# A hybrid decoder step's projections as Strassen products of seven for eight, over pairs of column tiles

## The chip, the cores and the metric

The kernel runs on one core of one Trainium2 chip. The metric is the device time of one execution in microseconds (us). Before the change it is 1708.05 us, the median of three runs (1707.87 to 1709.57). All data are fp32 in DRAM. A core has a matrix engine (TensorE, PE in the profile; PEld is its weight load), three engines for elementwise work (VectorE or DVE, ScalarE or ACT, GpSimd or POOL) and SyncE (SP), whose queue issues the DMAs here. Each engine runs its own list of instructions strictly in order; semaphores hold it where it needs another's result.

## The reference, cut to what matters

One inference step of a decoder layer, for 1024 prompt tokens and 8 x 4 sample tokens together (1056 columns):

```
h = rmsnorm(x, g_norm)                    # x: 1056 tokens x 2048
P = h @ w_in                              # 2048 x 5904: columns of groups A, B, C, D
y_a = b * conv3(c * h_a) * silu(z_a)      # A: gated short convolution
y_b = rmsnorm(gla(q, k, v, decay)) * silu(z_b)          # B: gated linear attention, 4 heads
y_c = window_attention(q, k, v, sinks) * silu(z_c)      # C: window 128, 8 heads on 2 key heads
y_d = softmax(q mem_k) mem_v * silu(z_d)  # D: 256 memory tokens, 4 heads
y = x + concat(y_a, y_b, y_c, y_d) @ w_out              # 2048 x 2048
```

For the prompt the memory's keys and values are `rmsnorm(mem) @ w_mem_kv`; for the samples they come from caches, as do the earlier keys and states. New states and caches are outputs too.

## The kernel before

**Tiles.** Features lie on the 128 partitions, tokens along the free axis. The two projections have 46 column tiles of P (four of each part of A and so on) and 16 of the output. A column tile is 128 rows of P transposed, [128, 1056], in three chunks of 352 columns (`CW`), one PSUM bank each. k has 16 tiles of 128.

**Precision.** An fp32 operand is split in a high and a low part, in a format (fp32r) that TensorE takes in one pass: x into `xh` and `xl` (`load_x`, `split`), weights into `wh` (ACT, L344) and `wl` (POOL, mostly, L348). Three matmuls, wh xh + wl xh + wh xl, stand for one exact one (`products`, L369). So a column tile is 16 x 3 x 3 matmuls of 352 columns. A plain fp32 matmul appears in the trace as two records.

**Normalisation.** x is multiplied by `g_norm` when it is split. Its row norm R is known only once all of x is there; it is multiplied in where a chunk leaves PSUM (`to`, L414; `silu2`, L425).

**Stages.** `first_two` does D's first two query tiles while x arrives. `memory` does the memory's keys and values (L491). Then `tile_of` and `proj` do tile after tile: D's queries, a quarter of A, D's gates, C's keys, values and queries, a quarter of A, C's gates, and B in two halves, each with a quarter of A. Each finished feature of the mixer goes to `mix` in DRAM; in the last gate tile (`last_gate`) it is loaded and split again (L281, L282), taking x's place, and `output` does 16 tiles with the residual (L1314).

**What sets the order.** Attention runs in generators that stand in a queue (`_Pipe`). One step of each active one is issued before every twelve matmuls of a projection (`pipe.step()` in `proj`), so twelve steps go with a column tile. `pipe.drain()` issues all steps that are left, with no products between. The compiler's scheduler then orders each engine's instructions anew. Weights come as pieces [128, 512], loaded and split two pieces ahead (`take`).

**Names that the steps below use.** D: scores L599, low parts L636, output L627; its decode takes the cached keys `kc` (L673, loads L668) and values `vc` (L704, loads L698). C: `c_duo` does two blocks of two heads, scores L863, mask and maximum L871, exponent L883, division L891, transposes L900, output L911; then `c_decode`. B: `b_duo`, `b_blocks`, and `b_decode`, in which each sample's keys are picked (L1289), multiplied (L1293) and added to the state (L1295). L257 sums squares of x, L285 makes the low part of x, L434 applies a gate on POOL.

Of the kernel before, what the change touches and what calls it, by code (L numbers as in the profile page):

```python
# [22 lines left out]
CW = TOK // NCH  # L23
CG = TOK // 4
# [5 lines left out]
# Column tiles of the combined projection, and where their 128 columns lie in w_in.  # L30
# [13 lines left out]
def _columns():  # L44
# [7 lines left out]
    for j in range(2):  # L52
# [7 lines left out]
# Mixer features in the order in which their tiles are done.  # L60
MIX = ["A0", "D0", "D1", "D2", "D3", "A1", "C0", "C1", "C2", "C3",
       "A2", "B0", "B1", "A3", "B2", "B3"]
# [12 lines left out]
class _Pipe:  # L75
    """Work that fills in between the projections' products, in stages: each of its generators
    yields where the tensor engine would wait for the other engines."""
# [4 lines left out]
    def add(self, gen, alone=False, after=None, every=0, kind=None):  # L82
        """after: what must hold something before the generator starts; every: steps between the
        starts of those of a kind."""
        self.queue.append((gen, alone, after, every, kind))

    def step(self):
        self.t += 1
        left = []
        for gen, phase, alone in self.active:  # L90
# [4 lines left out]
        self.active = left  # L95
# [14 lines left out]
class _Step:  # L110
    def __init__(self, nc, tc, ctx, I, O):
# [4 lines left out]
        self.xp = e(tc.tile_pool(name="xp", bufs=KT))  # L116
        self.wp = e(tc.tile_pool(name="wp", bufs=3))
        self.rt = e(tc.tile_pool(name="rt", bufs=7))
        self.ct = e(tc.tile_pool(name="ct", bufs=4))
        self.sm = e(tc.tile_pool(name="sm", bufs=3))  # L120
        self.pj = e(tc.tile_pool(name="pj", bufs=4, space=PS))
        self.ms = e(tc.tile_pool(name="ms", bufs=4, space=PS))
        self.mix = tc.dram_tile([KT, P, TOK], F32, name="mix")
# [3 lines left out]
        self.xh, self.xl = [None] * KT, [None] * KT  # L127

# [7 lines left out]
    def ctile(self):  # L136
        return self.ct.tile([P, CW], F32, name=self.name("ct"), tag="ct")

    def ps(self, pool=None):
        if pool is self.pj:  # L140
            return self.pj.tile([P, 512], F32, name=self.name("pj"), tag="pj")
        return self.ms.tile([P, 512], F32, name=self.name("ms"), tag="ms")
# [5 lines left out]
    def take_constants(self):  # L148
# [30 lines left out]
        self.R = c.tile([P, TOK], F32, name="R")  # L179
# [10 lines left out]
    def masks(self):  # L190
        nc, c = self.nc, self.const
        # decode: [cached key, t]
# [4 lines left out]
        # gated linear attention: all ones where s <= t  # L197
# [6 lines left out]
        # the same for the sample group's chunks of 4, and which chunk a token is of  # L204
# [16 lines left out]
    def rsqrt(self, out, x, mult, eps, n):  # L221
        """out = 1 / sqrt(x * mult + eps) for a few columns."""
# [21 lines left out]
    def load_x(self):  # L244
        """Splits x * g_norm into two parts that one pass each carries; sums the squares."""
        nc = self.nc
        self.acc = [None] * 2
        last = None

        def square(k, xr):  # L250
            i = int(k % 4 == 3)
            nc.scalar.activation(xr, xr, AF.Square)  # L252
            if self.acc[i] is None:
                self.acc[i] = xr
            else:
                eng = nc.vector if i else nc.gpsimd
                eng.tensor_tensor(self.acc[i], self.acc[i], xr, op=ALU.add)  # L257
        for k in range(KT):
            xr = self.rtile("xr")
            parts = 1 if k else NCH  # L260
            w = TOK // parts
            for c in range(parts):
                s = slice(c * w, c * w + w)
                nc.sync.dma_start(out=xr[:, s], in_=self.I["xT"][k, :, s])
            self.split(k, xr, self.gn[:, k : k + 1], parts)
            if last:
                square(*last)
            last = k, xr
# [4 lines left out]
    def split(self, k, src, scale=None, parts=1):  # L273
        nc = self.nc
        h = self.xp.tile([P, TOK], F32R, name=self.name("xh"), tag="xh")
        l = self.xp.tile([P, TOK], F32R, name=self.name("xl"), tag="xl")
        w = TOK // parts
        for c in range(parts):
            a, b, d = (t[:, c * w : c * w + w] for t in (src, h, l))
            if scale is None:  # L280
                nc.scalar.copy(b, a)  # L281
                nc.vector.tensor_tensor(d, a, b.bitcast(F32), op=ALU.subtract)  # L282
            else:
                nc.scalar.activation(b, a, AF.Copy, scale=scale)  # L284
                nc.vector.scalar_tensor_tensor(d, a, scale, b.bitcast(F32), op0=ALU.mult,  # L285
                                               op1=ALU.subtract)
        self.xh[k], self.xl[k] = h, l

    def row_norms(self):
        """R[:, t] = 1 / rms(x_t), on every partition."""  # L290
# [5 lines left out]
        ps = self.ps(self.pj)  # L296
        nc.tensor.matmul(ps[:, 0:2], acc[:, TOK - P : TOK], self.ones[:, 0:2], start=True, stop=True)
        r = self.small(NB + 1, tag="rx")
        self.rsqrt(r[:, 0:NB], sums, 1.0 / D_MODEL, EPS, NB)
        self.rsqrt(r[:, NB : NB + 1], ps[:, 0:1], 1.0 / D_MODEL, EPS, 1)  # L300
        for g in range(3):
            ps = self.ps(self.ms if g == 1 else self.pj)
# [9 lines left out]
    # Weights pass through in pieces of 512 columns, in the order of self.pieces, loaded and split  # L312
    # ahead of the products that take them.
    def load_piece(self):
        nc = self.nc
        kind, src = self.pieces[len(self.raw)]
        n = len(self.raw)
        if kind == "m":
            # two pieces in one go
            wr = self.rtile("wm")  # L320
            nc.sync.dma_start(out=wr[:, 0:1024], in_=src)
            self.raw += [wr[:, 0:512], wr[:, 512:1024]]
            return
        if n < 8 and n % 2:
            wr = self.t5()
        else:
            wr = self.wp.tile([P, 512], F32, name=self.name("wr"), tag="wr", bufs=2)
        nc.sync.dma_start(out=wr, in_=src)
        self.raw.append(wr)

    def split_piece(self):
        nc = self.nc
        n = len(self.ready)
        kind, wr = self.pieces[n][0], self.raw[n]
        # while x arrives, and for the memory, every other piece lies where attention will
        if n < 8 and n % 2:
            wh, wl = self.r5(), self.r5()
        elif kind == "m" and n % 2:
            wh, wl = self.t5().bitcast(F32R), self.t5().bitcast(F32R)
        else:  # L340
            wh = self.wp.tile([P, 512], F32R, name=self.name("wh"), tag="wh")
            wl = self.wp.tile([P, 512], F32R, name=self.name("wl"), tag="wl")
# [4 lines left out]
        eng = nc.vector if n < 8 or (kind == "m" and n % 2) else nc.gpsimd  # L347
        eng.tensor_tensor(wl, wr, wh.bitcast(F32), op=ALU.subtract)  # L348
        self.ready.append((wh, wl))

# [12 lines left out]
    def products(self, ps, wh, wl, kq, c, kk):  # L363
# [8 lines left out]
    def proj(self, evac, after=None):  # L372
        """One column tile; work of the pipe comes in between."""
        ps = []
        for kq in range(4):
# [9 lines left out]
            if after:  # L385
                after(kq)
# [1143 lines left out]
```

## Time and profile before

| | |
|---|---|
| runs of the kernel | 1707.87, 1708.05, 1709.57 us |
| the profiled execution | span 1708.3 us |
| mean granted TensorE clock | 0.993 |
| L369, high by high, 2928 records | 329 ns each (they overlap) |
| HBM read and written | 111.18 MB and 19.66 MB |
| largest wait of PE | 7.9 us, for kc |

The durations of matmuls are modelled and overlap, so the distance between two starts says what one costs. A line `L369 PE MATMUL out<-in shapes xcount | busy, mean ns | idle before, releaser` is a group of instructions of one source line.

### The profile page before, as it was taken

The page shows a single profiled execution, that of the slowest core. Times are in us where ns is not written, and L with a number is a line of the kernel's source. Part 1 is how long each engine was busy: PE and PEld are TensorE (multiplying, and loading weights), DVE is VectorE, ACT ScalarE, POOL GpSimd, SP SyncE. Part 2 cuts the span into 40 slices and gives each one's busy share as a digit, 9 for nine tenths or more (in the row PEclk, how much of TensorE's full clock was granted, in tenths as well). Part 3 has the DMA queues.
Part 4 walks back from the last instruction along what each step waited for, and adds up shares of the span by engine and source line. Part 5 has one row for each costly group of instructions (what it writes and reads, how often), then busy time and mean ns, then how long its engine had stood idle before and what let it go on. Part 6 is the DMA issues. An engine that isn't in the chain of part 4 may idle for free.

```text
span 1708.3 us, 26563 instructions
## 1 busy us (share of the span) xinstructions
PE 1666.3 (98%) x10850; PEld 1593.0 (93%) x10850; DVE 548.1 (32%) x1500; ACT 464.4 (27%) x1068; POOL 452.7 (26%) x351
## 2 busy tenths in 40 slices
PE   7889998999999999999999999999999999999999
PEld 6769987999999998989999989999989999999999
DVE  8865532111224544232512731112732600000000
ACT  7454431111125553111612421112422411111110
POOL 5441122233221111363222122322122422222221
PEclk9999998999999999999999999999999999999999
DMA  6441024322110112111111122111132722232221
GB/s 234 143 151 60 26 81 109 120 74 71 46 46 32 32 56 60 59 55 65 54 47 38 34 62 76 56 50 38 35 99 86 266 90 92 90 101 82 75 70 45
DMA packets 74446, 132.57 MB, mean 78 GB/s; under 512 B 14036, under 2 KB 31828, under 8 KB 74324
## 3 DMA queue, kind: packets, MB, share of 16 engines
q1 hardware_dynamic: 74324, 130.87, 23.9%
q8 instruction: 85, 1.39, 0.3%
q14 instruction: 37, 0.30, 0.1%
HBM read 111.18 MB, written 19.66 MB: 77 GB/s over the span
## 4 chain that ended last, share of the span: by engine, by line
PE 59%; ACT 1%; DVE 0%; issue 0%; ACTq 0%; DVEq 0%
PE pj L369 55%; PE ms L1030 1%; PE ms L1170 0%; PE ms L1167 0%; PE ms L1173 0%; PE ms L1222 0%; PE ms L1293 0%; PE ms L1197 0%; ACT L1057 0%; PE ms L1198 0%; PE ms L1083 0%; PE ms L1270 0%; DVE ct L427 0%; ACT ct L1055 0%; ACT ct L1058 0%
## 5 line engine op out<-in xcount | busy, mean ns | idle before, releaser
L369 PE MATMUL pj<-xh,wh 128*128 128x352 f32 x2928 | 963.7, 329 | 5.4 <-DVE wl L348 5.4
L369 PE MATMUL pj<-xl,wh 128*128 128x352 f32 x2928 | 942.9, 322 | 2.0 <-DVE xl L285 1.9
L369 PE MATMUL pj<-xh,wl 128*128 128x352 f32 x2928 | 942.3, 322 | 0.8 <-POOL wl L348 0.8
L348 POOL TENSOR_TENSOR wl<-wr,wh 128x512 fp32r<-128x512 f32 x240 | 319.8, 1333 | 1089.4 <-ACT wh L344 1021.1
L369 PEld LDWEIGHTS pj<-xh,wh 128*128 128x128 f32 x2928 | 551.0, 188 | 27.6 <-issue 19.2
L369 PEld LDWEIGHTS pj<-xl,wh 128*128 128x128 f32 x2928 | 550.7, 188 | 5.2 <-DVE xl L285 3.2
L369 PEld LDWEIGHTS pj<-xh,wl 128*128 128x128 f32 x2928 | 552.6, 189 | 1.5 <-POOL wl L348 1.0
L344 ACT CAST wh<-wr 128x512 fp32r<-128x512 f32 x243 | 150.6, 620 | 877.1 <-PE pj L369 805.9
L1314 DVE TENSOR_TENSOR xo<-pj,xo 128x352 f32<-128x352 f32 x48 | 25.2, 525 | 329.9 <-PE pj L369 329.9
L425 DVE TENSOR_TENSOR ct<-pj,R 128x352 f32<-128x352 f32 x48 | 25.1, 522 | 169.4 <-PE pj L369 169.4
L427 DVE SCALAR_TENSOR_TENSOR ct<-ct,ct 128x352 f32<-128x352 f32 x48 | 42.2, 880 | 23.1 <-ACT ct L426 23.1
L883 ACT ACTIVATE t<-t,sm,sm 128x256 f32<-128x256 f32 (+1 forms) x64 | 36.9, 577 | 43.7 <-DVE sm L875 43.7
L257 POOL TENSOR_TENSOR xr<-xr,xr 128x1056 f32<-128x1056 f32 x11 | 35.7, 3245 | 22.1 <-ACT xr L252 21.5
L426 ACT ACTIVATE ct<-ct 128x352 f32<-128x352 f32 x48 | 23.9, 497 | 53.8 <-DVE ct L425 52.1
L369 PE MATMUL ms<-xh,r 128*128 128x352 f32 x96 | 25.9, 346 | 10.6 <-DVE r L348 5.9
L285 DVE SCALAR_TENSOR_TENSOR xl<-xr,consts,xh 128x1056 fp32r<-128x1056 f32 (+1 forms) x18 | 34.9, 1968 | 3.4 <-ACT xh L284 3.4
L414 DVE TENSOR_TENSOR bv<-pj,R 128x352 f32<-128x352 f32 x12 | 6.3, 524 | 84.9 <-PE pj L369 84.9
L348 POOL TENSOR_TENSOR wl<-wm,wh 128x512 fp32r<-128x512 f32 x16 | 23.2, 1453 | 37.3 <-ACT wh L344 22.4
L491 PE MATMUL ms<-t,r 128*128 128x512 f32 x96 | 26.7, 402 | 3.6 <-DVE t L348 3.5
L369 PEld LDWEIGHTS ms<-xh,r 128*128 128x128 f32 x96 | 18.0, 201 | 12.6 <-DVE r L348 7.1
L753 DVE TENSOR_TENSOR ct<-pj,R 128x352 f32<-128x352 f32 x12 | 6.3, 524 | 69.1 <-PE pj L369 69.1
L491 PEld LDWEIGHTS ms<-t,r 128*128 128x128 f32 x96 | 17.5, 188 | 10.4 <-DVE t L348 6.5
(332 smaller groups left out, 1275.3 us busy)
## 6 DMA issues: line engine op xcount, KB each, us to landing
wr<-in_w_in SPq DMA_DIRECT2D x180, 256.0 KB
wr<-in_w_out SPq DMA_DIRECT2D x64, 256.0 KB
xo<-in_xT SPq DMA_DIRECT2D x16, 528.0 KB
out_yT<-xo SPq DMA_DIRECT2D x48, 176.0 KB
wm<-in_w_mem SPq DMA_DIRECT2D x16, 512.0 KB
xr<-in_xT SPq DMA_DIRECT2D x15, 528.0 KB
mx<-mix SPq DMA_DIRECT2D x14, 528.0 KB
kc<-in_cache_mem_kT SPq DMA_DIRECT2D x8, 512.0 KB
```

Source lines behind the costliest of these rows:

```text
L257: eng.tensor_tensor(self.acc[i], self.acc[i], xr, op=ALU.add)
L285: nc.vector.scalar_tensor_tensor(d, a, scale, b.bitcast(F32), op0=ALU.mult, op1=ALU.subtract)
L344: nc.scalar.copy(wh, wr)
L348: eng.tensor_tensor(wl, wr, wh.bitcast(F32), op=ALU.subtract)
L369: self.nc.tensor.matmul(ps[:, 0:CW], w[:, ks], x[:, cs], start=(k == 0 and i == 0), stop=(k == KT - 1 and i == len(pairs) - 1))
L425: nc.vector.tensor_tensor(z, ps, self.R[:, cs], op=ALU.mult)
L426: nc.scalar.activation(t, z, AF.Tanh, scale=0.5)
L427: nc.vector.scalar_tensor_tensor(z, t, 1.0, z, op0=ALU.add, op1=ALU.mult)
L491: nc.tensor.matmul(ps[t][c], a[:, ts], b, start=(k == 0 and i == 0), stop=(k == KT - 1 and i == 2))
L883: nc.scalar.activation(ps[u][:, g, kts[0] : 2], ps[u][:, g, kts[0] : 2], AF.Exp, bias=mx[:, c : c + 1], scale=rq[:, 4 * m + c : 4 * m + c ...
L1030: nc.tensor.matmul(ps[32 * j : 32 * j + 16, 0:CG], w[:, 16 * k : 16 * k + 16], x[:, j * CG : (j + 1) * CG], start=(k == 0), stop=(k == KT ...
L1314: nc.vector.tensor_tensor(x[:, cs], ps, x[:, cs], op=ALU.add)
```

## The change

**Seven products for eight.** Two column tiles and half of k make a 2 x 2 block product with two halves of the tokens (528 each, `H`): blocks [256 columns of W] x [512 of k] against [512 of k] x [528 tokens]. Strassen's product in Winograd's form needs seven products in place of eight, of sums of the blocks. The four halvings are: column tile (two), k in four quarters of 512 of which a phase takes two, and tokens. There are 23 pairs in the input projection less the one that `first_two` does, and 8 in the output; each runs in two phases, the first over k's first half, the second over its other half: 22 + 22 + 8 + 8 = 60 calls of `pair`. A product is 2 chunks x 4 k tiles x 3 matmuls of 264 columns (`CG`), so 168 to a pair and 10,080 in all.

**Sums of x (`strands`).** The seven right-hand operands, B11, T2, B21, T1, T3, B22, T4, are sums of x's quadrants, each [128, 4 x 528], and are split into high and low parts in SBUF (14 tiles). x is multiplied by `g_norm` and R first. Phase 0's strands are made in SBUF while the memory's products run (`first_strands`). Those of phase 1 and of the output's two phases are made as their features come (`second_x`, `feature`, `combine`), stored in DRAM, and loaded and split in the seven products of the last pair of the phase before (`strands`): three such switches.

**Sums of weights (`make_weights`).** Four DVE additions of 128 x 512 a pair, and seven splits; the low parts are DVE's in the input projection's phase 0 (calls 0 to 21) and POOL's after it (`heavy`).

**First sums in DRAM.** A pair's result of phase 0 is stored (`keep`) in the fourth product of the next pair, and loaded as `base` in phase 1. A pair leaves PSUM by DVE additions (L663), ACT copies and, with a base, three additions on POOL (L680, L693). Two-bank PSUM tiles are used in turn, with one product between an evacuation and the product that takes its banks.

**Order of work.** `pipe.step()` comes twice a product, so 14 steps to a pair. In phase 0 the pipe holds D's heads 0 and 1 and the second half of x; D's other heads and decode, C and B come in phase 1.

**Plain products.** D's output (L926 now) and C's scores (L1147) become one plain fp32 matmul instead of three fp32r ones, without their splits. The decay's first product is done with the normalised x (`rank`, L479).

```diff
-    def products(self, ps, wh, wl, kq, c, kk):
-        k = 4 * kq + kk
-        cs, ks = slice(c * CW, c * CW + CW), slice(kk * P, kk * P + P)
-        pairs = [(wh, self.xh[k]), (wl, self.xh[k]), (wh, self.xl[k])]
...
+    def split(self, i, src):
...
+        for n, x in enumerate(src):
+            s = slice(n * w, n * w + w)
+            nc.scalar.copy(h[:, s], x)
+            nc.vector.tensor_tensor(l[:, s], x, h[:, s].bitcast(F32), op=ALU.subtract)
...
+    def combine(self, ph, kk, f1, f2, eng):
+        to = self.xs[ph]
+        a, b, c, d = f1[:, 0:H], f1[:, H:TOK], f2[:, 0:H], f2[:, H:TOK]
...
+        eng.tensor_tensor(t3, d, b, op=ALU.subtract)
+        eng.tensor_tensor(b, b, a, op=ALU.subtract)
+        eng.tensor_tensor(t2, t3, a, op=ALU.add)
...
+        eng.tensor_tensor(t4, c, t2, op=ALU.subtract)
...
+    def make_weights(self):
...
+        elif i == 1:
...
+            v.tensor_tensor(s1, r(1, 0), r(1, 1), op=ALU.add)
+            v.tensor_tensor(s2, s1, r(0, 0), op=ALU.subtract)
...
+        wh, wl = self.weights()
+        nc.scalar.copy(wh, x)
+        eng.tensor_tensor(wl, x, wh.bitcast(F32), op=ALU.subtract)
...
+    def product(self, ps, i, first=True):
...
+        for c in range(2):
+            self.pipe.step()
+            for kk in range(4):
+                ks = slice(kk * P, kk * P + P)
+                xs = slice(kk * H + c * CG, kk * H + c * CG + CG)
+                for n, (w, x) in enumerate(((wh, sh), (wl, sh), (wh, sl))):
+                    nc.tensor.matmul(ps[:, 512 * c : 512 * c + CG], w[:, ks], x[:, xs],
...
+    def pair(self, fin, base=None, strands=None, at_once=None):
...
+        x, y = self.two(), self.two()
+        self.product(x, B11)
+        u = self.htile("u")
+        nc.scalar.copy(two(u), bank(x))
+        after(0)
+        self.product(y, T2)
+        add(u, u, y)
+        if base:
+            for o in (out[0][1], out[1][0]):
+                nc.gpsimd.tensor_tensor(o, o, u, op=ALU.add)
+        after(1)
+        self.product(x, B21, False)
...
+        z = self.two()
+        self.product(z, T1)
...
+        w = self.two()
+        self.product(w, T3)
+        add(out[1][1], out[1][1], w)
+        after(4)
+        self.product(z, B22, False)
+        add(out[0][1], out[0][1] if base else u, z)
+        after(5)
+        self.product(w, T4, False)
+        add(out[1][0], out[1][0] if base else u, w)
...
-            for i, (a, b) in enumerate(((self.vmh, ph), (self.vml, ph), (self.vmh, pl))):
...
+            nc.tensor.matmul(op[:, 0:256], self.vm[:, t, h * P : h * P + P],
+                             p[:, 256 * t : 256 * t + 256], start=(t == 0), stop=(t == 1))
...
-            for i, (a, b) in enumerate(((qh, self.kh), (qh, self.kl), (ql, self.kh))):
...
+                                 q[r, n * P : n * P + P], self.kg[r, ks], start=True, stop=True)
```

**What moved on the engines.** On TensorE, before, within C's attention: products (L369) lie around a duo's transposes (L900), and twelve and more of them come before its output.

```order
L369 MATMUL pj_4556<-xl_341,wh_4533 128x352
L369 MATMUL pj_4556<-xh_366,wh_4533 128x352
L369 MATMUL pj_4556<-xh_366,wl_4534 128x352
L369 MATMUL pj_4556<-xl_367,wh_4533 128x352
L900 MATMUL ms_4755<-ident,t_4644 128x128 x2
L900 MATMUL ms_4759<-ident,t_4645 128x128 x4
L369 MATMUL pj_4576<-xh_288,wh_4533 128x352
L369 MATMUL pj_4576<-xh_288,wl_4534 128x352
L369 MATMUL pj_4576<-xl_289,wh_4533 128x352
```

On TensorE, now, at the end of C's attention, where the pipe is drained: outputs of duos (L1195), sums of squares and transposes (L865, L872: the decode's), transposes of other duos (L1184) and scores (L1147) follow each other, with products (L644) before and behind.

```order
L644 MATMUL pj_10807<-s_6572,wh_10251 128x264
L644 MATMUL pj_10807<-s_6572,wl_10252 128x264
L1195 MATMUL ms_10423<-t_10272,vcur 64x128 x4
L1195 MATMUL ms_10423<-t_10273,vcur 64x128 x4
L865 MATMUL ms_10435<-sq_10420,blk_102 32x256 x4
L1184 MATMUL ms_10442<-ident,t_10368 128x128 x4
L1184 MATMUL ms_10448<-ident,t_10369 128x128 x4
L872 MATMUL ms_10454<-ident,t_10440 128x128 x2
L1147 MATMUL ms_10479<-kg,d_9052 128x128
L1147 MATMUL ms_10480<-kg,d_9052 128x128
L1147 MATMUL ms_10479<-kg,d_9052 128x256
L1147 MATMUL ms_10480<-kg,d_9052 128x256
```

The products that stood between one step of a duo and its next are gone from this place.

On VectorE, before, at the change from the input projection to the output's: the last features are split (L282) among the last gate's work (L425, L427), and then the residual is added (L1314).

```order
L282 TENSOR_TENSOR xl1924_12853<-mx1922_12850,xh1923_12852 128x1056
L427 SCALAR_TENSOR_TENSOR ct1930_12892<-ct1931_12893,ct1930_12892 128x352
L425 TENSOR_TENSOR ct1932_12910<-pj1882_12687,R_103 128x352
L282 TENSOR_TENSOR xl1936_12919<-mx1934_12916,xh1935_12918 128x1056
L427 SCALAR_TENSOR_TENSOR ct1932_12910<-ct1933_12911,ct1932_12910 128x352
```

On VectorE, now, at the last of the three switches, within the output: strands are split (L426) between evacuations (L663), and sums of weights follow (L618, L604).

```order
L663 TENSOR_TENSOR d2601_16771<-pj2633_16944,d2601_16771 128x528
L426 TENSOR_TENSOR s2637_16975<-sx2622_16893,s2636_16974 128x1056
L426 TENSOR_TENSOR s2645_17018<-sx2631_16938,s2644_17017 128x1056
L663 TENSOR_TENSOR d2600_16770<-pj2623_16895,d2600_16770 128x528
L426 TENSOR_TENSOR s2645_17018<-sx2632_16940,s2644_17017 128x1056
L426 TENSOR_TENSOR s2653_17061<-sx2638_16980,s2652_17060 128x1056
L663 TENSOR_TENSOR d2601_16771<-pj2633_16944,d2601_16771 128x528
L426 TENSOR_TENSOR s2653_17061<-sx2639_16982,s2652_17060 128x1056
L426 TENSOR_TENSOR s2662_17103<-sx2646_17023,s2661_17102 128x1056
L426 TENSOR_TENSOR s2662_17103<-sx2647_17025,s2661_17102 128x1056
L618 TENSOR_TENSOR wr2625_16898<-wr2625_16898,ws2649_17028 128x512
L604 TENSOR_TENSOR ws2680_17271<-wr2641_16986,wr2668_17170 128x512
```

One split of all features once has become a split of seven strands three times, in the queue in which the evacuations stand.

On GpSimd, before, within the output: low parts of weights (L348), four to a column tile, and nothing else.

```order
L348 TENSOR_TENSOR wl1953_12991<-wr1945_12943,wh1952_12990 128x512
L348 TENSOR_TENSOR wl1956_13033<-wr1951_12988,wh1955_13032 128x512
L348 TENSOR_TENSOR wl1959_13075<-wr1954_13030,wh1958_13074 128x512
L348 TENSOR_TENSOR wl1963_13125<-wr1957_13072,wh1962_13124 128x512
L348 TENSOR_TENSOR wl1969_13170<-wr1961_13122,wh1968_13169 128x512
```

On GpSimd, now, in a pair of the output's second phase: seven low parts (L623) and three additions to the base (L680, L693) to two column tiles and half of k.

```order
L623 TENSOR_TENSOR wl2834_18533<-wr2789_18168,wh2833_18532 128x512
L680 TENSOR_TENSOR d2824_18464<-d2824_18464,u2830_18498 128x528
L680 TENSOR_TENSOR d2825_18465<-d2825_18465,u2830_18498 128x528
L623 TENSOR_TENSOR wl2839_18568<-wr2809_18332,wh2838_18567 128x512
L623 TENSOR_TENSOR wl2843_18602<-wr2808_18330,wh2842_18601 128x512
L693 TENSOR_TENSOR d2825_18465<-d2825_18465,v2840_18595 128x528
L623 TENSOR_TENSOR wl2845_18631<-wr2816_18398,wh2844_18630 128x512
L623 TENSOR_TENSOR wl2849_18664<-ws2847_18660,wh2848_18663 128x512
L623 TENSOR_TENSOR wl2855_18699<-wr2837_18564,wh2854_18698 128x512
L623 TENSOR_TENSOR wl2858_18729<-ws2846_18659,wh2857_18728 128x512
```

The additions of a pair stand between the low parts that its later products take.

More of the change, by code (lines that the diff above doesn't have):

```diff
@@ L23 @@
 CW = TOK // NCH
+H = TOK // 2
 CG = TOK // 4
@@ L271, in load_x, with row_norms @@
             yield k
[L273 to L289, printed above, removed]
+    def row_norms(self, spare):
         nc = self.nc
@@ L1432, in run @@
[L1432 to L1446 removed]
+                    for n, two in enumerate(self.two_in):
+                        if n == 8:
+                            pipe.add(self.second_x())
+                        last = n == len(self.two_in) - 1
+                        self.pair(self.keep(self.kept(two)), None, self.strands(1) if last else None)
```

803 lines of the change are left out of this document (475 added, 328 removed).

## The prediction

> **What bounds the kernel now.** I read the page's busy shares first, then the chain, then the trace by windows.
>
> ```profile
> span 1708.3 us, 26563 instructions
> PE 1666.3 (98%) x10850; PEld 1593.0 (93%) x10850; DVE 548.1 (32%) x1500; ACT 464.4 (27%) x1068; POOL 452.7 (26%) x351
> PE pj L369 55%; PE ms L1030 1%; PE ms L1170 0%; PE ms L1167 0%; PE ms L1173 0%; PE ms L1222 0%; PE ms L1293 0%; PE ms L1197 0%; ACT L1057 0%; PE ms L1198 0%; PE ms L1083 0%; PE ms L1270 0%; DVE ct L427 0%; ACT ct L1055 0%; ACT ct L1058 0%
> 0.00:43.00 43.00, 30.33 (x164) 27.64 (x165) 34.80 (x30) 30.85 (x36) 24.01 (x19) 0.96 0.69 233
> 43.00:85.00 42.00, 36.17 (x195) 31.64 (x194) 35.45 (x54) 20.36 (x32) 20.82 (x9) 0.92 0.45 145
> 85.00:128.00 43.00, 38.23 (x161) 28.46 (x160) 27.42 (x37) 21.91 (x39) 21.29 (x19) 1.00 0.45 149
> 500.00:600.00 100.00, 100.00 (x791) 92.74 (x791) 51.59 (x237) 50.31 (x144) 15.72 (x12) 1.00 0.10 33
> 1400.00:1500.00 100.00, 100.00 (x631) 100.00 (x630) 7.87 (x15) 11.18 (x18) 22.49 (x18) 1.00 0.29 92
> ```
>
> TensorE is busy 98% of the span, and the projection's L369 leads the chain. A window row gives its length, then the busy time of PE, PEld, DVE, ACT and POOL, the clock, DMA share and GB/s. Between 500 and 600 us C's attention costs DVE 51.59 and ACT 50.31 us, and PE is still full: products hide it. Only the first 128 us are not PE's: 104.7 us busy, with DVE at 97.7. The span is 1708.3 and the median of the runs 1708.05, so no correction lies between them.
>
> **Products.** Of the 8928 L369 matmuls, 8640 go (60 tiles x 16 k x 3 chunks x 3; the first two tiles' 288 stay). 10,080 come (30 pairs x 2 phases x 7 products x 24) with 264 columns for 352. Between 1400 and 1500 us 631 matmuls take 100 us: 158.5 ns each. Shorter ones run in D:
>
> ```profile
> 236.00 0.28 PE L627 MATMUL ms<-r,vmh 128*128 128x256 f32 x1
> 236.11 0.28 PE L627 MATMUL ms<-r,vml 128*128 128x256 f32 x1
> 236.23 0.40 PE L627 MATMUL ms<-r,vmh 128*128 128x256 f32 x2
> 236.47 0.28 PE L627 MATMUL ms<-r,vml 128*128 128x256 f32 x1
> 236.59 0.28 PE L627 MATMUL ms<-r,vmh 128*128 128x256 f32 x1
> 236.71 0.27 PE L618 MATMUL ms<-ident,t 128*128 128x128 f32 x1
> L369 PEld LDWEIGHTS pj<-xh,wh 128*128 128x128 f32 x2928 | 551.0, 188 | 27.6 <-issue 19.2
> ```
>
> Six matmuls of 256 columns start within 0.71 us: 118.3 ns each. Between 256 and 352 columns a column costs 0.42 ns, so 264 columns come to 121.7 ns. Then 10,080 x 0.1217 = 1227 against 8640 x 0.1585 = 1369: **-143 us**. Strict proportion (118.9 ns) would make it -171; I keep 121.7, next to the measured row.
>
> **Plain products in attention.** D's output and C's scores become one plain fp32 matmul, two records, for three in fp32r.
>
> ```profile
> 233.19 1.03 PE L599 MATMUL ms<-kTm,dq 128*128 128x256 f32 x4
> L599 PE MATMUL ms<-kTm,dq 128*128 128x256 f32 x64 | 16.4, 379 | 0.0
> 564.86 0.38 PE L863 MATMUL ms<-kh,r 64*128 64x256 f32 x2
> 565.56 0.28 PE L863 MATMUL ms<-kh,r 64*128 64x256 f32 x2
> 567.78 1.03 PE L900 MATMUL ms<-ident,t 128*128 128x128 f32 x8
> ```
>
> Four L599 records take 1.03 us, of which the last is 0.379: 217 ns apart. D: 64 records for 96, 64 x 0.217 - 96 x 0.118 = +2.5. In C two heads' scores run at once: of a duo's six pairs the first starts at 564.86 and the sixth at 565.56, 0.14 us apart, and about 0.118 without the first step. 84 such pairs become 56 of 0.217: +2.2. Together **+5**; the splits that go with it were hidden.
>
> **The start.** While the memory's products run, seven strands have to be made of x.
>
> ```profile
> L282 DVE TENSOR_TENSOR xl<-mx,xh 128x1056 fp32r<-128x1056 f32 x14 | 19.8, 1440 | 4.9 <-PE pj L369 2.8 <-ACT xh L281 2.1
> L285 DVE SCALAR_TENSOR_TENSOR xl<-xr,consts,xh 128x1056 fp32r<-128x1056 f32 (+1 forms) x18 | 34.9, 1968 | 3.4 <-ACT xh L284 3.4
> L257 POOL TENSOR_TENSOR xr<-xr,xr 128x1056 f32<-128x1056 f32 x11 | 35.7, 3245 | 22.1 <-ACT xr L252 21.5
> L348 DVE TENSOR_TENSOR t<-wm,t 128x512 fp32r<-128x512 f32 x16 | 17.1, 1082 | 6.3 <-ACT t L344 3.9 <-PE ms L491 2.3
> ```
>
> DVE gains eight 1056-wide normalising steps (as 16 halves), 14 subtractions of 1056, eight sums of 1056, 11 sums of squares from POOL, and the memory's other 16 low parts: 8 x 1.97 + 33 x 1.44 + 16 x 1.08 = 81 us. Against this POOL, free of its 11 sums of 3.2 us, takes seven first low parts from DVE, and DVE's steps beside it get shorter: some 25 us off, as an estimate. DVE's 97.7 become about 154 in 128, but the last strands may lie beside pair 0. I take **+12** (0 to +30).
>
> **The three strand switches.** In a phase's last pair seven strands are loaded and split, each 2 x 540 KB.
>
> ```profile
> GB/s 234 143 151 60 26 81 109 120 74 71 46 46 32 32 56 60 59 55 65 54 47 38 34 62 76 56 50 38 35 99 86 266 90 92 90 101 82 75 70 45
> ```
>
> The best slice moved 266 GB/s, so 7.57 MB need 28 us, and a pair has 168 x 0.1217 = 20.4. DVE's 14 splits of 1.44 cost 20 us beside some 11 of its usual work; behind a split stand evacuations, and the product after next needs their banks. Either way about 8 us are late, if the next pair's strands cannot wait: 3 x 8 = **+24** (10 to 60).
>
> **Attention with less cover.** All of C and B and half of D now run in phase 1, where a tile's products are half of k: 10.2 us instead of 22.8 (144 x 0.1585). The order of PE shows groups of attention with few or no products between.
>
> ```profile
> PE ms L673 <- DMA kc<-in_cache_mem_kT: 7.9, 1, 7.9
> 262.00:272.00 10.00, 7.28 (x49) 6.36 (x48) 4.43 (x8) 2.10 (x4) 1.50 (x1) 0.96 0.31 22
> 272.00:282.00 10.00, 4.83 (x22) 4.03 (x23) 0.00 (x0) 0.82 (x2) 1.28 (x1) 0.52 0.62 162
> kc<-in_cache_mem_kT SPq DMA_DIRECT2D x8, 512.0 KB
> vc<-in_cache_mem_v SPq DMA_DIRECT2D x8, 512.0 KB
> 562.03 1.14 DVE L891 TENSOR_SCALAR t<-t,sm 128x256 f32<-128x256 f32 x4
> 565.98 0.42 DVE L871 CUSTOM_DVE_ANT_0 t<-ms,mband 128x256 f32<-128x256 f32 x1 [2.81 <-PE ms L863]
> 571.40 1.14 DVE L891 TENSOR_SCALAR t<-t,sm 128x256 f32<-128x256 f32 x4
> L1289 DVE TENSOR_SCALAR bw<-bw,own 32x128 f32<-32x128 f32 x16 | 6.0, 376 | 0.4 <-ACT bw L1261 0.3
> L1295 DVE SCALAR_TENSOR_TENSOR s<-s,bw,ms 128x128 f32<-128x128 f32 x16 | 5.5, 345 | 10.7 <-PE ms L1293 10.7
> ```
>
> D's decode loads 16 x 512 KB; some 98 products (12 us) and about 15 us of its own matmuls lie beside that. 8.4 MB take 32 us at 266 GB/s, 52 at 162: +5 to +25, **+12**, since the first loads run ahead. On SP they wait for buffers that PE frees, and the next pair's weights stand behind them. A wait costs twice: beside the 7.9 us the window's clock is 0.52. [...]
>
> C: a duo's DVE steps run from 565.98 to 572.54, 6.6 us, and its output waits for them. At C's end two duos and the decode, about four such chains (26 us), have 114 products (14 us) beside them: +12 to +26, more if duos keep their old period of 9.4 us (571.40 less 562.03); I take **+20**. B: each of the 16 samples waits through 0.376 + 10.7 / 16 + 0.345 = 1.4 us, with six to ten products (0.7 to 1.2) between; with its block chain I take **+10** a group, +20 (0 to 45).
>
> **The steady pairs** should run at PE's pace.
>
> ```profile
> L348 POOL TENSOR_TENSOR wl<-wr,wh 128x512 fp32r<-128x512 f32 x240 | 319.8, 1333 | 1089.4 <-ACT wh L344 1021.1 <-issue 68.2
> L636 DVE TENSOR_TENSOR r<-ms,r 128x512 fp32r<-128x512 f32 x16 | 11.0, 686 | 8.2 <-ACT r L635 8.2
> L434 POOL TENSOR_TENSOR cq<-cq,ct 128x352 f32<-128x352 f32 x12 | 11.3, 945 | 11.2 <-DVE ct L427 11.2
> L1314 DVE TENSOR_TENSOR xo<-pj,xo 128x352 f32<-128x352 f32 x48 | 25.2, 525 | 329.9 <-PE pj L369 329.9
> L427 DVE SCALAR_TENSOR_TENSOR ct<-ct,ct 128x352 f32<-128x352 f32 x48 | 42.2, 880 | 23.1 <-ACT ct L426 23.1
> ```
>
> From pair 22 on POOL has 7 x 1.333 + 3 x 1.42 (945 ns for 352 columns, so 1.42 us for 528) = 13.6 us in 20.4. DVE has four sums at 0.686 and six evacuations at 0.79 (525 x 1.5): 7.5. A DVE step with both operands in SBUF takes longer beside POOL (L427, 880, with L1314 at 525): 4 x 0.36 more, 9 in all. So a buffer slips now and then only; with POOL's sums of features (32 of 1.42 us, four to a pair) I put **+8** (0 to 20). The first sums' way through DRAM costs nothing: 1.1 to 2.2 MB of loads and stores, with 1 MB of weights, in 20.4 us are 104 to 157 GB/s, and at 92 the DMA engines are busy 0.29. If that cover goes, it is in the switches.
>
> **Sum:** 1708.3 - 143 + 5 + 12 + 24 + 12 + 20 + 20 + 8 = **1666 us**, -2.5%.
>
> **Rivals.** (a) *Attention sets the pace in phase 1*, on the slower side. C's 16 duos have four pairs of products beside them (82 us) and some 38 of their own matmuls: 12 of scores, 120 transposes at 0.109 ((1.03 - 0.27) / 7 in the row above), and as an estimate as much for the outputs. They fit if a duo takes under 120 / 16 = 7.5 us. Their old period is 9.4, and DVE and POOL now carry more beside them. At 10.4, a little over the old period, it is 16 x 2.9 = +46 for C, 26 above the forecast; 20 more for each group of B, at the end of its range, and D's decode at 162 GB/s (+25 for +12) give 1666 + 26 + 40 + 13 = 1745. For it: DVE 51.59 in a window that has more cover. Against it: that period was set by the steps, not by any engine at its limit. (b) *The stalls stay hidden*: the reorder fills them, as at 500 to 600 us; only the start, the small terms and one late switch remain: 1708 - 143 + 5 + 12 + 8 = 1590. (c) *The change does not do what it says*, since loading weights sets the rate: PEld is busy 100.00 of 100 us. Then 10,080 x 0.1585 = 1598 and the time is 1937 before any stall. Against it: L627 has a load for each matmul and runs at 118 ns, though a load's record is 188. The Trainium skill (Perfetto Trace Analysis, Identifying the Most-Contended Engine) would judge PE's headroom by the busy share of LDWEIGHTS; by that rule this rival is the likelier, and the L627 rows speak against it. (d) *The losses cancel the gain*: they are 101 in the sum, and at 143, well within their bounds, nothing is left.
>
> **Chances:** forecast 0.56 (1630 to 1700), (a) 0.20, (b) 0.17, (c) 0.02, (d) 0.05. The range from 1600 to 1740 leaves out half of (a), half of (b), and (c), 0.20 in all. 0.2% (3.4 us) is about what a measurement of this kernel can tell from no change; forecast, (b) and the low end of (a) (0.03) make faster 0.76, same 0.05, slower 0.19.
>
> **What would show it.** L644 near 122 ns apart in windows without attention; PE idle before the products in the pairs after each switch, released by DVE; waits of kc and vc in D's decode; in C and B waits of PE for t and bw on DVE. If PE is full there, (b) holds. If L644 is 158 ns apart, (c). If DVE or ACT is over 80% busy in C's windows, (a).

## The result and the profile after

The changed kernel takes 1794.4 us (median of four runs, 1791.8 to 1804.3) against 1708.4: a ratio of 1.051, 95% interval 1.048 to 1.054. It is slower, where 1666 us and a range of 1600 to 1740 were forecast.

The page of the changed kernel, its busy row and its chain:

```profile
span 1792.3 us, 31152 instructions
PE 1607.7 (90%) x12194; PEld 1507.3 (84%) x12194; DVE 1082.3 (60%) x2100; ACT 649.8 (36%) x1372; POOL 624.6 (35%) x463
PE 61%; DVE 18%; DMA 6%; issue 5%; ACT 5%; POOL 5%; SPq 0%; DVEq 0%; ACTq 0%; POOLq 0%
```

PE has less to do (1608 us busy for 1666) and stands for 184.6 us, before for 42. VectorE, which had no share in the chain, has 18%. The clocks of the two kernels, from the view of the cores, before first:

```profile
core 0: 1708.3 us, clock 0.993
```

```profile
core 0: 1792.3 us, clock 0.950
```

Of 1792 us, 5.0% are clock that was not granted: 90 us, where before it was 12. So the account is: before 1708 = 1654 of work at full clock + 42 idle + 12 of clock; after 1792 = 1518 + 184 + 90. Some of the clock fell away while PE stood idle anyway (14 of the 90 us, 6 of the 12), and this account takes it twice; with it taken once, the work is 1531 after 1660. **The work fell by 129 to 136 us, where 138 were forecast. Idle time and clock rose by some 220, where 96 were forecast.**

Where they are is seen in three windows of the changed kernel (columns as before: length, PE, PEld, DVE, ACT, POOL, clock, DMA share, GB/s): steady pairs of phase 0, attention of D in phase 1, steady pairs of the output.

```profile
250.00:300.00 50.00, 50.00 (x415) 50.00 (x414) 25.10 (x37) 13.03 (x22) 0.00 (x0) 1.00 0.28 98
700.00:750.00 50.00, 37.56 (x253) 29.48 (x253) 24.95 (x46) 15.29 (x42) 17.94 (x19) 0.85 0.37 127
1500.00:1550.00 50.00, 50.00 (x414) 50.00 (x413) 15.97 (x23) 11.56 (x19) 33.69 (x27) 1.00 0.44 146
```

Steady pairs run without a gap, with POOL idle in phase 0 and with POOL busy 34 of 50 us in the output: 414 matmuls in 50 us are 120.8 ns each. Between 700 and 750 no engine but PE is busy even half of the time on average, and yet PE waits 12.4 us and has 0.85 of its clock. In shorter stretches VectorE is nearly full:

```profile
1260.00:1280.00 20.00, 12.26 (x69) 12.09 (x70) 18.64 (x41) 9.75 (x19) 11.61 (x9) 0.77 0.17 54
```

Added over all windows of 10 us, 222 of the 274 us of loss lie between 660 and 1500 us, phase 1 and the start of the output.

What PE, and then VectorE, waited for in the changed kernel:

```profile
PE pj L644 <- DVE d L663: 27.4, 18, 5.3
PE ms L1184 <- DVE t L1175: 16.7, 15, 2.3
PE ms L1484 <- ACT bw L1479: 15.7, 6, 5.6
PE ms L919 <- DVE t L913: 15.6, 10, 4.5
PE pj L644 <- ACT u L674: 15.0, 4, 4.5
PE pj L644 <- POOL wl L623: 11.9, 7, 2.4
```

```profile
DVE d L663 <- POOL d L693: 79.3, 24, 8.9
```

There are many waits of 1 to 5 us, on VectorE for the most part: of PE's 179 us of waits, 107 end with VectorE, 53 with ScalarE and 13 with POOL. And VectorE itself stands 79 us before an evacuation (L663) because POOL's addition (L693) to the same tile is late. A stretch of VectorE's timeline in the changed kernel, and POOL's beside it:

```profile
1089.52 7.83 DVE L1328 TENSOR_TENSOR_SCAN cum<-ones,la 128x64 f32<-128x64 f32 x16
...
1099.08 0.69 DVE L663 TENSOR_TENSOR d<-pj,d 128x528 f32<-128x528 f32 x1
1099.70 2.24 DVE L1384 TENSOR_TENSOR bw<-cum 128x256 f32<-128x256 f32 x1
1101.86 1.27 DVE L1396 COPY sm<-bw 128x2 f32<-128x2 f32 x1
```

```profile
1090.09 2.58 POOL L680 TENSOR_TENSOR d<-d,u 128x528 f32<-128x528 f32 x2
1092.63 1.28 POOL L623 TENSOR_TENSOR wl<-wr,wh 128x512 fp32r<-128x512 f32 x1
1094.45 1.29 POOL L623 TENSOR_TENSOR wl<-wr,wh 128x512 fp32r<-128x512 f32 x1 [0.54 <-ACT wh L622]
...
1099.23 2.43 POOL L736 TENSOR_TENSOR d<-d,d 128x1056 f32<-128x1056 f32 x1 [3.48 <-DVE d L727]
1101.74 1.37 POOL L520 TENSOR_TENSOR t<-d,d 128x528 f32<-128x528 f32 x1
```

Sixteen scans take 7.83 us while POOL works most of the time (3.02 us in the kernel no_pool, below), and a copy of 128 x 2 takes 1.27, nearly as long as the POOL step beside it. The evacuation stands behind the scans, and PE waits 3.3 us for it.

### The profile page after: what moved, and what is told of

It reads as the page before. It is cut to its first block, busy times and chain, and to the rows that moved or that the text cites. A ratio compares the mean times of both kernels' runs of the same rounds, so it can differ in the third digit from the quotient of the medians.

```text
span 1792.3 us, 31152 instructions
## 1 busy us (share of the span) xinstructions
PE 1607.7 (90%) x12194; PEld 1507.3 (84%) x12194; DVE 1082.3 (60%) x2100; ACT 649.8 (36%) x1372; POOL 624.6 (35%) x463
## 4 chain that ended last, share of the span: by engine, by line
PE 61%; DVE 18%; DMA 6%; issue 5%; ACT 5%; POOL 5%; SPq 0%; DVEq 0%; ACTq 0%; POOLq 0%
PE pj L644 53%; POOL wl L623 2%; DVE s L426 2%; DMA wr<-in_w_in 1%; DVE d L663 1%; DVE t L1175 1%; PE ms L793 1%; DMA x<-in_xT 1%; POOL d L680 1%; DVE sm L265 1%; DMA wr<-in_w_mem 1%; ACT t L1167 1%; DVE cum L1328 1%; DMA wr<-in_w_out 1%; PE ms L1147 1%
## 5 line engine op out<-in xcount | busy, mean ns | idle before, releaser
L644 PE MATMUL pj<-s,wh 128*128 128x264 f32 x6720 | 1311.1, 293 | 59.2 <-DVE d L663 27.4
L644 PEld LDWEIGHTS pj<-s,wh 128*128 128x128 f32 x6720 | 1087.3, 195 | 83.9 <-issue 39.9
L644 PE MATMUL pj<-s,wl 128*128 128x264 f32 x3360 | 978.4, 291 | 11.9 <-POOL wl L623 11.9
L644 PEld LDWEIGHTS pj<-s,wl 128*128 128x128 f32 x3360 | 654.8, 195 | 15.8 <-POOL wl L623 13.4
L623 POOL TENSOR_TENSOR wl<-wr,wh 128x512 fp32r<-128x512 f32 x190 | 260.3, 1372 | 744.6 <-ACT wh L622 739.6
L663 DVE TENSOR_TENSOR d<-pj,d 128x528 f32<-128x528 f32 x174 | 122.2, 704 | 215.0 <-PE pj L644 135.4
L623 POOL TENSOR_TENSOR wl<-ws,wh 128x512 fp32r<-128x512 f32 x76 | 103.4, 1360 | 206.8 <-ACT wh L622 206.6
L622 ACT CAST wh<-ws 128x512 fp32r<-128x512 f32 x120 | 74.6, 622 | 133.6 <-PE pj L644 128.4
L680 POOL TENSOR_TENSOR d<-d,u 128x528 f32<-128x528 f32 x76 | 105.1, 1403 | 7.5 <-DMA wr<-in_w_out 5.8
L623 DVE TENSOR_TENSOR wl<-wr,wh 128x512 fp32r<-128x512 f32 x110 | 75.9, 690 | 45.3 <-ACT wh L622 45.3
L604 DVE TENSOR_TENSOR ws<-wr,wr 128x512 f32<-128x512 f32 x60 | 45.3, 754 | 72.4 <-DMA wr<-in_w_in 39.3
L663 DVE TENSOR_TENSOR u<-pj,u 128x528 f32<-128x528 f32 x60 | 42.3, 704 | 77.0 <-PE pj L644 76.1
L663 DVE TENSOR_TENSOR d<-pj,u 128x528 f32<-128x528 f32 x66 | 46.6, 706 | 50.7 <-PE pj L644 50.7
L674 ACT COPY u<-pj 128x528 f32<-128x528 f32 x60 | 35.8, 597 | 97.3 <-PE pj L644 96.3
L426 DVE TENSOR_TENSOR s<-sx,s 128x1056 fp32r<-128x1056 f32 x42 | 69.3, 1675 | 0.8 <-ACT s L425 0.7
L663 DVE TENSOR_TENSOR v<-pj,u 128x528 f32<-128x528 f32 x38 | 26.7, 704 | 63.1 <-PE pj L644 63.1
L693 POOL TENSOR_TENSOR d<-d,v 128x528 f32<-128x528 f32 x38 | 52.2, 1373 | 27.1 <-DVE v L663 12.4
L618 DVE TENSOR_TENSOR wr<-wr,ws 128x512 f32<-128x512 f32 x60 | 45.5, 759 | 23.0 <-POOL wl L623 22.4
L425 ACT CAST s<-sx 128x1056 fp32r<-128x1056 f32 x42 | 44.6, 1071 | 16.5 <-PE pj L644 9.6
```

Source lines behind the costliest of these rows:

```text
L425: nc.scalar.copy(h[:, s], x)
L426: nc.vector.tensor_tensor(l[:, s], x, h[:, s].bitcast(F32), op=ALU.subtract)
L604: v.tensor_tensor(s1, r(1, 0), r(1, 1), op=ALU.add)
L618: v.tensor_tensor(x, x, self.wsum[n][1], op=ALU.subtract)
L622: nc.scalar.copy(wh, x)
L623: eng.tensor_tensor(wl, x, wh.bitcast(F32), op=ALU.subtract)
```

## The experiments

Two theories stood after this. *C*: attention and evacuations, in order on VectorE, have too few products beside them (rival (a) of the prediction). *P*: GpSimd's work in phase 1 is the cause. Losses below are idle time and clock together, from each run's profile. The kernels no_attn, block_after, block_before, lock and no_pool_attn were run once each.

**light**, the low parts of the weights on VectorE throughout:

```diff
     def heavy(self, n):
-        return n >= 22
+        return False
```

> Low parts of the weights on VectorE everywhere, none on GpSimd after the start. Theory P (GpSimd's low parts lengthen VectorE's steps through the shared access to SBUF, and low parts of weights come late behind sums on GpSimd): the waits of PE for POOL wl (11.9 us) go, VectorE's small steps beside GpSimd fall from over 1.2 us to 0.2, and the idle and half-clock time between 660 and 1500 us, 222 us, falls by 60 or more: 1735 us or less. Theory C (attention's own chains and evacuations in order on VectorE have too few products beside them): VectorE gets 4.8 us a pair more, so no gain, 1780 to 1815.

1723.0 us, ratio 1.0097 (1.0081 to 1.0114). It is 71 us less, though VectorE was busy 98 us longer. That is P's number. The loss falls from 274 to 198 us.

**no_attn**, the changed kernel without the attention of phase 1:

```diff
-                for h in (2, 3):
-                    self.d_head(q[h], h)
-                pipe.add(self.d_decode(q), alone=True)
...
-                    self.c_head(j, q[j])
-                    self.c_head(j + 1, q[j + 1])
-                pipe.add(self.c_decode(pool, q))
...
-                self.group_b(pool, i, cum, kq[1], kq[0], v)
```

> Left out: in phase 1 the attention of D's heads 2 and 3, the sample decode of D, all of C's scores to outputs (its keys and values stay) and all of B's linear attention; gates, convolution, decay, feature sums and products stay. Theory C: the losses (idle and half clock, 222 us between D's second queries and the output) fall to 70 or less, which are the pairs with gates and decay; with the left-out matmuls (about 130 us at full clock) the time is about 1510. Theory P: the low parts and sums on GpSimd are as before, so at least 120 us of loss stay: 1560 or more.

1539.7 us, and 163 us of loss, 118 of them between 600 and 1250 us, with no attention there. The time lies between the two numbers and the loss just under P's bound of 120, far from C's 70. So attention is not the whole of it; but 111 us of loss went with it, so neither theory stands alone.

**block_after** and **block_before**, scans that nobody needs, among the evacuations:

```diff
         self.product(w, T3)
+        if self.wdone // 7 in (12, 14, 16, 18):
+            self.block(w, (528, 1056, 2112, 3168)[(self.wdone // 7 - 12) // 2])
...
+    def block(self, ps, n):
+        v = self.nc.vector
+        for a in range(0, n, TOK):
+            junk = self.rtile("junk")[:, 0 : min(TOK, n - a)]
+            v.memset(junk, 0.0)
+            v.tensor_copy(junk[:, 0:1], ps[:, 0:1])
+            v.tensor_tensor_scan(junk, junk, junk, 0.0, op0=ALU.mult, op1=ALU.add)
```

> Four needless blocks on VectorE, in pairs 12, 14, 16 and 18 of phase 0, where nothing else disturbs: scans of 528, 1056, 2 x 1056 and 3 x 1056 columns, started when the fifth product is done (2.3, 4.6, 9.2, 13.8 us, as an estimate from 0.295 us for 64 columns less the fixed part). Theory S (an evacuation may be late by one product of 2.9 us, then PE stands): the first costs nothing, the second under 1 us, the third 4 to 6, the fourth 8 to 11, and half clock on top of the last two. If evacuations had more room: nothing for the first three.

> The same four blocks in the output tiles 4, 6, 8 and 10 of the kernel before, started when a tile's first chunk is done. Theory S: its evacuations come three in 6 us and then none for 17, with 5.7 us of room: the first two blocks cost nothing, the third under 3 us, the fourth 5 to 8. If the room were the same as in the changed kernel: the same costs as there.

The scans took half of the estimate: 1.25, 2.35, 4.6 and 6.9 us (7.9 in the kernel before). In the changed kernel the pairs with them and behind them are 0, 0.8, 1.8 and 4.9 us longer, and 1.6 us by the clock behind the last; in the kernel before PE waits 0, 0, 0 and 2.9 us. The scheduler did not keep the larger blocks whole in the changed kernel: an evacuation stands between two scans of the third and of the fourth. What can be compared is scans in one piece: the kernel before hides 4.6 us of them and pays 2.9 for 7.9, the changed kernel pays 0.8 for 2.35. So theory S has the signs, and the new evacuations have less room, by some three microseconds; that makes VectorE's delays felt, but does not make them.

**lock**, as light, and POOL does each subtraction once more for nothing:

```diff
+        if n >= 22:
+            junk = self.htile("junk")[:, 0:512]
+            nc.gpsimd.tensor_tensor(junk, x, wh.bitcast(F32), op=ALU.subtract)
         self.wready.append((wh, wl))
```

> As light (low parts on VectorE), and from call 22 on GpSimd does the same subtraction once more into a tile that nothing reads: GpSimd is as busy as in the changed kernel, but nothing waits for its low parts. Theory L (it is GpSimd's occupancy of the shared access that lengthens VectorE's steps with two operands in SBUF): the gain of light is gone, 1780 us or more. Theory W (the low parts themselves came late in GpSimd's queue): 1735 or less.

1856.7 us, 134 above light. Late low parts are not the reason here, since VectorE makes them; POOL's being busy is what costs. It still held back the additions that VectorE waits for (47.5 us), and ScalarE and VectorE waited 48 us for buffers that the needless step read. Beside this flaw of the test, two ways were open: VectorE's own steps get longer (L), or VectorE waits in its queue for POOL's additions (Q).

**light_comb**, then **no_pool**, both with light's edit, step by step all of POOL's work after the start on VectorE:

```diff
-            for _ in self.combine(2 + k // 8, k % 4, *two, self.nc.gpsimd):
+            for _ in self.combine(2 + k // 8, k % 4, *two, self.nc.vector):
...
-                self.nc.gpsimd.tensor_tensor(o[i], o[i], z[i], op=ALU.mult)
+                self.nc.vector.tensor_tensor(o[i], o[i], z[i], op=ALU.mult)
...
-            nc.gpsimd.tensor_tensor(y[0], y[0], b, op=ALU.mult)
+            nc.vector.tensor_tensor(y[0], y[0], b, op=ALU.mult)
```

```diff
-                nc.gpsimd.tensor_tensor(o, o, u, op=ALU.add)
+                nc.vector.tensor_tensor(o, o, u, op=ALU.add)
...
-            nc.gpsimd.tensor_tensor(out[1][1], out[1][1], w, op=ALU.add)
+            nc.vector.tensor_tensor(out[1][1], out[1][1], w, op=ALU.add)
```

> As light, and the gates' products, the convolution's last product and the sums of features (L736, L1044, L520 to L528) on VectorE too; GpSimd keeps the three additions of a pair with a base. Theory L: the stalls in the pairs after the gates (26, 27, 33, 34, 39, 43, 44: 95 us in light) shrink by half, 1680 to 1700 us. If VectorE's own load is the limit there (it gains some 40 us of work): 1715 to 1740.

> As light_comb, and a pair's three additions to the base on VectorE too: GpSimd does nothing after the start. Theory L: every VectorE step runs at its own length, steady pairs keep 20.4 us with VectorE at some 14 us, and the time is 1670 to 1695 us. If VectorE's queue is the limit: slower than light_comb, above 1700, with waits for d L663 in steady pairs.

light_comb takes 1675.5 us, ratio 0.980 (0.977 to 0.984), from two runs 9 us apart. no_pool takes 1639.7 us, **ratio 0.960 (0.958 to 0.962)**: it is faster than the kernel before and the changed one. Both times are below L's numbers. The page of no_pool:

```profile
span 1636.3 us, 30856 instructions
PE 1559.1 (95%) x12194; PEld 1466.8 (90%) x12194; DVE 1186.7 (73%) x2528; ACT 650.3 (40%) x1372; POOL 26.0 (2%) x35
```

VectorE is busy longer than in any kernel above save lock, and the loss is 108 us. The steps that it shares with the changed kernel are shorter. Groups of the changed kernel (line, shapes, count, busy time, mean), then of no_pool:

```profile
L426 DVE TENSOR_TENSOR s<-sx,s 128x1056 fp32r<-128x1056 f32 x42 | 69.3, 1675 | 0.8 <-ACT s L425 0.7
L1175 DVE TENSOR_SCALAR t<-t,sm 128x256 f32<-128x256 f32 x56 | 27.5, 550 | 0.4
L1328 DVE TENSOR_TENSOR_SCAN cum<-ones,la 128x64 f32<-128x64 f32 x32 | 15.6, 559 | 0.0
L663 DVE TENSOR_TENSOR d<-pj,d 128x528 f32<-128x528 f32 x174 | 122.2, 704 | 215.0 <-PE pj L644 135.4
```

```profile
L426 DVE TENSOR_TENSOR s<-sx,s 128x1056 fp32r<-128x1056 f32 x42 | 51.6, 1249 | 2.5 <-ACT s L425 2.4
L1175 DVE TENSOR_SCALAR t<-t,sm 128x256 f32<-128x256 f32 x56 | 16.1, 350 | 0.3
L1328 DVE TENSOR_TENSOR_SCAN cum<-ones,la 128x64 f32<-128x64 f32 x32 | 6.0, 269 | 0.0
L663 DVE TENSOR_TENSOR d<-pj,d 128x528 f32<-128x528 f32 x174 | 122.6, 705 | 98.2 <-PE pj L644 97.3
```

In these groups a step within SBUF takes 1.3 to 2.1 times as long with POOL beside it; an evacuation out of PSUM (L663) is 0.704 or 0.705 us. Over all groups that both kernels have, the changed kernel's steps are 157 us longer in sum.

**tables**, as no_pool, with the decay's exponent and logarithm each once over all columns:

```diff
-                t = self.htile("t")[:, 0:CG]
-                nc.scalar.activation(t, ps[:, 0:CG], AF.Abs, bias=b)
...
-                nc.scalar.activation(t, t, AF.Exp, scale=-1.0)
-                nc.scalar.activation(t, t, AF.Ln, bias=1.0)
-                nc.vector.tensor_tensor(la[:, cs], la[:, cs], t, op=ALU.subtract)
+                nc.scalar.activation(t[:, cs], ps[:, 0:CG], AF.Abs, bias=b)
...
+            nc.scalar.activation(t, t, AF.Exp, scale=-1.0)
+            yield
+            nc.scalar.activation(t, t, AF.Ln, bias=1.0)
+            yield
+            nc.vector.tensor_tensor(la, la, t, op=ALU.subtract)
```

> As no_pool, and the decay's exponent and logarithm each once over all 1056 columns instead of four times over 264, so that ScalarE loads two tables for them in place of some seven (1.28 us each) ahead of the evacuation copies that stand in its queue. If those loads are what PE waits for in pairs 34 and 39 (ACT u L674, 8.8 us in two waits, and half clock): 10 to 20 us under no_pool. If not: within 4 us of it.

1637.0 us (0.958, 0.956 to 0.959): not told apart from no_pool. But this does not clear the table loads. In no_pool PE waits twice for ScalarE's copy (L674), 4.3 us each, in pairs 34 and 39; in tables those two waits are gone, and in the same pairs PE waits 6.9 and 7.0 us for an evacuation on VectorE (L663). One wait has taken the other's place. PE's waits in no_pool, then in tables:

```profile
PE pj L644 <- ACT u L674: 12.9, 4, 4.3
PE pj L644 <- DVE d L663: 7.2, 14, 1.1
```

```profile
PE pj L644 <- DVE d L663: 19.6, 12, 7.0
PE pj L644 <- ACT u L674: 3.5, 2, 2.0
```

**lock2**, as no_pool, with the needless subtraction of lock on POOL, so that VectorE waits for nothing of POOL's; and **adds_dve**, the changed kernel with L680 and L693 on VectorE (the second diff of no_pool alone):

> As no_pool (1640 us, nothing on GpSimd after the start), and from call 22 on GpSimd does each low part's subtraction once more into a tile that nothing reads, so that nothing on VectorE waits for a result of GpSimd. Theory L (beside a GpSimd step VectorE's steps with operands in SBUF take longer: 157 us in all in the changed kernel over no_pool): 1710 us or more, with L426 and L1328 about as long as in the changed kernel (1.68 and 0.56 us). Theory Q (in VectorE's queue an evacuation waits for GpSimd's addition, which stands behind low parts: d L663 <- POOL d L693, 79.3 us): within 10 us of no_pool.

> As the changed kernel, low parts on GpSimd from call 22, but a pair's three additions to the base (L680, L693) on VectorE. Theory Q: no evacuation waits for GpSimd any more, 1690 us or less. Theory L: GpSimd is still busy 9.3 us in a pair with low parts, VectorE's steps stay long and VectorE has 2.1 us more: 1750 to 1800. Half of each: 1700 to 1750.

lock2: 1783.5 us, ratio 1.043 (1.040 to 1.047), 144 above no_pool. From its page:

```profile
PE 1598.5 (90%) x12194; PEld 1495.3 (84%) x12194; DVE 1382.8 (78%) x2528; ACT 650.9 (37%) x1372; POOL 459.8 (26%) x301
```

VectorE's steps are the same as there, and it is busy 196 us longer (1382.8 us against 1186.7), some 130 of them in steps that the changed kernel has too (L426 1429 ns, L1331, the same scan, 329, less than was expected). Some of the 144 is a wait of my making: ScalarE stood 34.6 us, in 14 waits, for a buffer that POOL's needless step still read. PE's waits tell how much of that can have reached it: against no_pool those that end with VectorE grow by 81 us, those that end with ScalarE by 21. What VectorE itself lost by ScalarE's lateness is not separated. So L is borne out, and Q is not needed for most of the cost.

adds_dve: 1751.9 us, 1.025 (1.023 to 1.027), 42 us below the changed kernel and at the near end of L's range. No evacuation waits for POOL any more, so Q alone would have given 1690 or less. The 42 us are not the price of that wait alone: VectorE has 121 us more to do there, and its other steps, with POOL less busy, are some 46 us shorter. The low parts, gates and sums on POOL are worth the other 112.

**before_dve**, the kernel before with its weights' low parts on VectorE:

```diff
-        eng = nc.vector if n < 8 or (kind == "m" and n % 2) else nc.gpsimd
+        eng = nc.vector if n < 8 or kind == "w" or n % 2 else nc.gpsimd
```

> The kernel before with all low parts of the projections' weights on VectorE instead of GpSimd. Both theories: its products hide either, since PE was busy 98%; within 6 us of 1708. If it gained as the changed kernel does, the gain of no_pool would not be the change's own.

1702.5 us, 0.996 (0.9945 to 0.9974): the same step that gave the changed kernel 71 us gives the old one 6 or 7. Its products hid POOL.

**no_pool_attn**, no_pool without phase 1's attention (the edit of no_attn):

> As no_pool, with the same attention of phase 1 left out as in no_attn (D's heads 2 and 3 and decode, C's scores to outputs, B's linear attention). no_pool loses 108 us to idle and half clock, 68 of them between 600 and 1400 us; no_attn against the changed kernel says that the left-out matmuls are some 140 us at full clock. If attention with less cover is what is left of the losses (52 us as forecast): 1440 to 1460 us. If the decay, the gates and the switches are: 1480 or more.

1465.3 us, in between: the left-out matmuls weigh more than the 140 us taken. The losses say it better: 92 us against 108 in no_pool. With POOL quiet, attention loses 16 us. C's attention alone shows the same. Its stretch in the changed kernel, then in no_pool:

```profile
870.00:1032.00 162.00, 137.97 (x1103) 117.82 (x1101) 122.52 (x379) 83.50 (x239) 56.01 (x44) 0.93 0.20 64
```

```profile
826.00:962.00 136.00, 133.74 (x1148) 116.23 (x1146) 116.35 (x429) 84.73 (x242) 2.57 (x3) 1.00 0.25 78
```

PE stands 24 us there with POOL at work and 2 us without, although VectorE's busy share is higher without (86% for 76%).

## Why the prediction was wrong

- **Products: right.** Forecast 121.7 ns each, measured 120.8; all of PE's work at full clock falls by 129 to 136 us, forecast 138. Rival (c), with 158 ns, is out; so are (b), which hid the stalls, and (d), whose losses of 143 us the rise of 220 passes.
- **The step that failed** is "The steady pairs should run at PE's pace", where POOL was put at **+8** (0 to 20). The steady pairs do run so. But POOL's load was weighed there alone, on four sums of weights a pair. What POOL lengthens are VectorE's steps within SBUF wherever the two meet, and in phase 1 those are attention's, the decay's and the gates' too. Measured: 1794 less 1640 in no_pool, 155 us, in place of 8. The row for it stood in the prediction (L427, 880 ns beside 525), and was applied to four sums a pair, 1.4 us more, instead of to the whole queue. That VectorE's evacuation would wait for POOL's addition behind low parts was not seen at all; VectorE stands 79.3 us so, and to move the additions gains 42 us net (adds_dve). How the 155 us divide between longer steps and late additions is not shown to the microsecond; lock2 says that the longer steps are the larger part.
- **The clock** has no term of its own in the sum; the prediction names it only beside D's decode. In the changed kernel 90 us of clock are lost, in 34 stretches at half clock, behind waits that are shorter than the one long wait (7.9 us) the trace of before had. The Trainium skill (TensorE: Matmul & The Clock Gate, HAM oscillation) describes this cost for waits longer than a window of some 3.4 us. Here a wait of 1.84 us was enough, as the last section shows, so the measurement decides.
- **Attention with less cover**, +52 with D, C and B. With POOL busy, leaving attention out saves 111 us of loss; with POOL quiet 16. So there was cover enough for VectorE's undisturbed steps, and rival (a) had the sign right and the wrong cause: it made the halved cover the price, and it is only what the delay needs to be felt. Its mark, DVE or ACT over 80% busy in C's windows, told nothing: over C's stretch VectorE is busy 76% in the changed kernel, and 86% in no_pool, where C loses almost nothing.
- **Start and switches**, +12 and +24. By the trace the memory's last product starts at 139.3 us, before at 125.6: +14. Of the switches the last stands alone, in the output: 4.0 us of loss in pair 51 and 4.5 in the two after it, where 8 was the price of each. That this agrees is in part luck: in no_pool the same three pairs lose 2.9 us, so most of it is POOL's too.
- **The rest of the sum**: without POOL's term the forecast is 1658, and no_pool, the nearest run to that case, takes 1640.

## What to carry to other kernels

Before work is spread to an engine that has room, ask which other engine's steps lengthen beside it, and apply that factor to everything in the other's queue, in the stage where that queue matters. Mean busy shares do not show it: in C's stretch VectorE had the higher busy share in the kernel that lost almost nothing there, and moving all work from a POOL busy 35% to a VectorE busy 60% made the kernel 8.6% faster. When a change halves the cover of side work, chains that cost nothing before are priced anew, with the clock that each wait costs.

## What the runs showed of the hardware

A POOL step delays not only VectorE steps with two operands in SBUF: a copy of 128 x 2 took 1.27 us beside it (0.16 in no_pool), and L1175, one tile and a column of scalars, 550 ns for 350.

The clock falls behind waits far shorter than the 7.9 us of the kernel before. Windows of the changed kernel, 3.4 us each:

```profile
1605.20:1608.60 3.40, 1.56 (x13) 1.36 (x12) 3.40 (x2) 2.96 (x4) 3.40 (x3) 1.00 0.01 3
1608.60:1612.00 3.40, 3.40 (x17) 3.40 (x17) 3.40 (x4) 0.00 (x0) 3.40 (x2) 0.50 0.77 218
1612.00:1615.40 3.40, 3.40 (x29) 3.40 (x29) 3.40 (x3) 2.58 (x3) 3.40 (x3) 0.99 1.04 393
```

A single wait of 1.84 us, in which PE was idle for just over half of one such stretch, is followed by 3.4 us at half clock: 17 matmuls ran where 29 did in the next. The wait cost 1.84 us, and the clock 1.7 more. Of the 34 stretches at half clock in this kernel, 33 come behind 3.4 us in which PE was idle for 1.38 us or more in all.
